# Adding the feed forward's residual with accumulating DMAs that queue behind GpSimd's gate products

## The chip, the cores and the metric

One core of a Trainium2 chip runs the whole program. Its engines are TensorE (PE, with its weight loads as PEld), VectorE (DVE), ScalarE (ACT), GpSimd (POOL) and SyncE (SP); each works off a queue of its own, in order. The metric is device time in microseconds, lower is better; it is the median of several executions.

## The reference, cut to what matters

Two layers work on 512 latent tokens of 1024 features (and 256 context tokens in layer 0). Each layer ends in a feed forward whose result is gated, feature by feature, and added to the residual:

```python
x = x + g1 * y
x = x + g2 * swiglu(modulate(x, norm_ffn_g[i], sh2, sc2), ffn_w_gate[i], ffn_w_up[i], ffn_w_down[i])
# swiglu(h) = (silu(h @ w_gate) * (h @ w_up)) @ w_down, with 2816 hidden features
```

In layer 0 the context tokens take the same path with gates of their own. In layer 1 a final RMSNorm follows.

## The kernel before

Every float32 product is made of three float32r products of high and low parts (`mm3`, L149 to L151). The feed forward's 2816 hidden features are 22 blocks of 128, numbered m = 0 to 21, and are made in pairs. A pair m, m + 1 goes through `up_strassen`: `W.strassen` loads four weight tiles (two of the gate matrix, two of the up matrix) into the ring `raw` of four buffers, GpSimd makes sums and differences in place in them (L116 to L119, one set of four for the gate matrix and one for the up matrix), and ScalarE and VectorE split each into a high part (L106) and a low part (L107). That gives seven left factors for each matrix. TensorE multiplies them into `p`, twelve matmuls for each factor; VectorE adds the products up in `a` (L888). Then ScalarE takes the silu, and L891 multiplies by the up half: for the first m of a pair on GpSimd, for the second on VectorE. `parts` splits the result for the down product (L842, L843).

The down product runs in sections: nine sections of one pair, then a last section of two pairs, m = 18 to 21. A section's sums `pd` are added by VectorE to an accumulator that stays in SBUF (L931). In the last section the first four sums begin with m = 18 and 19 alone ("the ahead groups": 24 matmuls that don't need the last pair), and each finished sum goes to `finish`, where it is gated and added.

Between the pairs, `between(m)` is called. At m = 18, behind the products of that pair in the program text and ahead of the last pair (20, 21), the kernel turns the accumulator of the nine sections into gate times accumulator plus residual. This is `ada_between` in layer 0 (L944, six tiles of 128 x 1024, the residual loaded from DRAM into the ring `raw`) and `settle` in layer 1 (L1435, four tiles, the residual in SBUF). Each tile takes a product on GpSimd (L951, L1438) and a sum on VectorE (L952, L1439). In layer 0, blocks of 16 small products for the modulation of layer 1 (`ada`, L230) fill TensorE between the pairs; their weights use the ring `raw` as well.

The order of every engine's queue is laid down when the program is built, by a planner that plays the program through on a model and, of the instructions that are ready for an engine, takes the one that stands first in the program text. From the last section's down product on, TensorE keeps the order of the text (`on_pe`). What the planner laid down does not change on the chip: an engine whose next instruction isn't ready waits.

Of the kernel before, what the change touches and what calls it, by code (L numbers as in the profile page):

```python
# [9 lines left out]
F32 = mybir.dt.float32  # L10
F32R = mybir.dt.float32r
AF = mybir.ActivationFunctionType
ALU = mybir.AluOpType
AX = mybir.AxisListType
PSUM = bass.MemoryType.PSUM

P = 128
# [37 lines left out]
class Weights:  # L55
    """Streams [128, 1024] weight units from DRAM and splits each into two float32r parts."""
# [5 lines left out]
    def slot(self):  # L62
        """[128, 1024] of the pools in turn"""
        pool, tag = self.pools[self.at // 2 % len(self.pools)], ("whi", "wlo")[self.at % 2]
        self.at += 1
        return pool.tile([P, 1024], F32R, tag=tag, name=f"w{self.at}")
# [28 lines left out]
    def strassen(self, pairs, order, eng):  # L95
        """The seven left factors of Winograd's form of Strassen's product, each [128, 512] in two parts, for pairs of units whose halves
        are the blocks (A11, A12) and (A21, A22); allotted in the given order of (pair, factor)"""
# [30 lines left out]
def kernel(ctx: ExitStack, tc: tile.TileContext, x, c, ctx_in, c_ctx, ada_w, ada_b,  # L128
# [24 lines left out]
    # constants and vectors  # L153
# [57 lines left out]
    def ada_steps(layer, ja, jb, ch, pp, slots=None):  # L211
        """256 features of two of the six parts of silu(c) @ ada_w + ada_b, feature on the partition of mod[layer, j].
        Column group k % 4 of the array sums the products of every fourth k."""
# [47 lines left out]
    def rms(xt, junk, n, name):  # L261
        """1 / sqrt(mean of squares + eps) of each row"""
# [13 lines left out]
    def norm_steps(xt, v, layer, j, dst, name):  # L276
        """modulate(xt) with parts j (shift) and j + 1 (scale), transposed, in two float32r parts: dst, each [128, 8, 128],
        or lists of its halves. First the norm, then the turning, in two halves"""
# [23 lines left out]
    def norm_later(*a):  # L302
        """the norm now, the turning when turn_oldest comes to it"""
        g_ = norm_steps(*a)
        next(g_)
        lag.append(g_)
# [6 lines left out]
    def on_pe():  # L313
        """from here the tensor engine keeps to the order in which its instructions are given"""
# [12 lines left out]
    class PP:  # L327
        """One PSUM pool under several tags."""
# [21 lines left out]
    # the first norm and the keys and values, as the shift and scale of each 256 features come in  # L350
# [16 lines left out]
    def h_chunk(ch):  # L367
        """features 256 * ch and on of the modulated, transposed tokens"""
# [50 lines left out]
    def rope(ps, t, nh, name):  # L419
        """rotated rows of a [128, nh*64] PSUM block"""  # L420
# [21 lines left out]
    def kv_evac(t):  # L442
        """keys (rotated) and values of token tile t out of PSUM, the keys in two float32r parts, each twice"""
# [9 lines left out]
    def k_turn(t, pools):  # L453
        """and turned"""
# [65 lines left out]
    def scores(t, b, h0, nh):  # L520
        """steps: masked scores of nh heads from h0 on of half b, query tile t, with the sink's logit behind them, and their maximum"""
# [39 lines left out]
    def weights(t, b, h0, nh):  # L561
        """their softmax weights"""
# [18 lines left out]
    def values(t, b, h0, nh):  # L581
        """their weighted values, feature on the partition: steps that turn the weights of some keys and steps that use them"""
# [45 lines left out]
    # what fills the array between the units: the coming queries and the modulation of the feed forward  # L628
# [115 lines left out]
    def add_gated(xt, ps, gate, hf, tmp, name):  # L744
        """xt[:, half] += gate * ps"""
# [5 lines left out]
    class Blocks:  # L751
        """The transposed tokens in 2 x 2 blocks (halves of the features, halves of the tokens, tile by tile), [128, 4, columns], each in
        two float32r parts; then what Winograd's form of Strassen's product takes in place of one of them, and three more"""
# [18 lines left out]
        def factors(self, more, tmp):  # L772
            """the seven right factors: B11, B21, B22 stay, more takes three, and B12 - B11, kept in the first two of tmp,
            is to take the place of B12"""
# [52 lines left out]
    def ffn(layer, h, extra, acc, xt, gate, es, sections, order, between, up_done, finish, mid):  # L827
# [18 lines left out]
        def up_first():  # L846
            """the first two m, one half of the tokens before the other"""
# [22 lines left out]
        def up_strassen(m):  # L870
            """m and m + 1: of each product's four blocks the first is P1 + P2, the second P1 + P6 + P5 + P3, the third P1 + P6 + P7 + P4,
            the fourth P1 + P6 + P7 + P5"""
# [16 lines left out]
            for x_, (g_, u_) in enumerate(a):  # L889
                nc.scalar.activation(out=g_, in_=g_, func=AF.Silu)  # L890
                (nc.vector if x_ else nc.gpsimd).tensor_tensor(out=u_, in0=u_, in1=g_, op=ALU.mult)  # L891
# [3 lines left out]
        for si, size in enumerate(sections):  # L895
# [22 lines left out]
            # the last section's first groups begin with the older half of the features  # L918
# [14 lines left out]

    es_x = ExitStack()
# [9 lines left out]
    def ada_between(m):  # L944
        if m == 4:
            G2.extend(load_gate(0, 5, 2))
        if m == 18:
            for e, t in enumerate((4, 5, 0, 1, 2, 3)):
                r = raw.tile([P, D], F32, tag="raw", name=f"xr_{t}")
                nc.sync.dma_start(out=r, in_=x_mid[t])  # L950
                nc.gpsimd.tensor_tensor(out=xt[t], in0=xt[t], in1=G2[0 if t < NL else 1], op=ALU.mult)  # L951
                nc.vector.tensor_tensor(out=xt[t], in0=xt[t], in1=r, op=ALU.add)  # L952
# [5 lines left out]
    def after_attention(e):  # L958
        """the turning of the last tiles behind the first products that don't need them"""
# [73 lines left out]
    def dt_step():  # L1033
        """step sizes of every head, their running sums along each chunk and what follows from them"""
# [434 lines left out]
```

## Time and profile before

| | us |
|---|---|
| three executions | 1975.98, 1976.86, 1983.81 |
| median | 1976.86 |
| span of the profiled execution | 1982.3 |
| longest of the three, the only one above that span | 1983.81 |
| TensorE busy | 1868.1 |
| VectorE busy | 1377.4 |
| GpSimd busy | 740.0 |

The span is the time from the first instruction to the last of one profiled execution. Of the times shown only 1983.81 can hold a span of 1982.3, so that is taken as its own time, with 1.5 us around the span. The feed forward of layer 0 ends its last pair at about 895 to 934 us, that of layer 1 at about 1920 to 1953 us.

### The profile page before, as it was taken

How to read it: one execution, taken by the hardware profiler on the slowest of the kernel's cores; microseconds unless marked ns; L12 is line 12 of the kernel's file. 1: busy time of each engine (PE TensorE's matmuls, PEld its weight loads, DVE VectorE, ACT ScalarE, POOL GpSimd, SP SyncE). 2: the span in 40 equal slices, each digit the busy share in tenths (PEclk: the TensorE clock that was granted, in tenths of full speed). 3: DMA queues.
4: the chain of work that ended last, by engine and by line, in shares of the span. 5: the costliest groups of instructions: out<-in, count | busy, mean ns of one | idle time of the engine just before them, and what ended most of it. 6: DMA issues, size and time to landing. Idle time of an engine off the chain costs nothing.

```text
span 1982.3 us, 29492 instructions
## 1 busy us (share of the span) xinstructions
PE 1868.1 (94%) x11168; PEld 1586.5 (80%) x11168; DVE 1377.4 (69%) x2359; ACT 894.2 (45%) x1607; POOL 740.0 (37%) x688
## 2 busy tenths in 40 slices
PE   6999998999999999989999999989989989999987
PEld 3777766889888888878888878777767888999877
DVE  4656655484666666687758777787777587787886
ACT  4675555344222222223556545665462454344333
POOL 1010002243333333364405545444545244535364
PEclk8999999999999999999999999999989999999989
DMA  9302137332333333344523332323243324332321
GB/s 303 119 1 86 43 98 240 121 117 86 106 107 106 107 107 107 107 132 144 162 75 110 96 87 81 112 85 105 85 157 103 113 86 123 91 107 85 107 59 70
DMA packets 226717, 214.88 MB, mean 108 GB/s; under 512 B 10352, under 2 KB 195152, under 8 KB 226576
## 3 DMA queue, kind: packets, MB, share of 16 engines
q1 hardware_dynamic: 214304, 189.56, 31.6%
q10 hardware_dynamic: 12272, 23.44, 3.4%
q8 instruction: 88, 1.44, 0.3%
q14 instruction: 53, 0.43, 0.1%
HBM read 201.27 MB, written 11.70 MB: 107 GB/s over the span
## 4 chain that ended last, share of the span: by engine, by line
PE 47%; DVE 16%; POOL 10%; DMA 10%; issue 9%; ACT 6%; ACTq 0%; POOLq 0%; DVEq 0%; SPq 0%
DVE w L107 4%; DMA R<-cum_rows 3%; PE p L149 3%; PE p L151 3%; PE p L150 3%; PE pd L149 3%; PE pd L150 2%; PE pd L151 2%; PE po L612 2%; POOL al L843 2%; DVE w L84 2%; PE ptp L596 2%; DMA raw<-in_ffn_w_gate_dram 2%; PE ada L230 2%; POOL raw L116 1%
## 5 line engine op out<-in xcount | busy, mean ns | idle before, releaser
L107 DVE TENSOR_TENSOR w<-raw,w 128x512 fp32r<-128x512 f32 x280 | 265.6, 962 | 138.8 <-ACT w L106 138.2
L106 ACT CAST w<-raw 128x512 fp32r<-128x512 f32 x280 | 166.2, 619 | 372.7 <-POOL raw L117 111.0
L149 PE MATMUL pd<-w,ah 128*128 128x512 f32 x440 | 175.1, 398 | 13.6 <-DVE y L931 9.0
L84 DVE TENSOR_TENSOR w<-raw,w 128x1024 fp32r<-128x1024 f32 (+1 forms) x117 | 152.2, 1304 | 34.0 <-ACT w L83 33.4
L150 PE MATMUL pd<-w,ah 128*128 128x512 f32 x440 | 173.5, 394 | 0.0
L83 ACT CAST w<-raw 128x1024 fp32r<-128x1024 f32 (+1 forms) x121 | 126.1, 1045 | 100.3 <-DMA raw<-in_ffn_w_down_dram 31.7
L151 PE MATMUL pd<-w,al 128*128 128x512 f32 x440 | 162.1, 394 | 4.2 <-POOL al L843 4.2
L149 PE MATMUL p<-hF_lh,w 128*128 128x256 f32 x384 | 110.7, 290 | 13.5 <-DVE ah_f L888 10.2
L149 PEld LDWEIGHTS pd<-w,ah 128*128 128x128 f32 x440 | 83.2, 189 | 35.6 <-DVE y L931 12.1
L116 POOL TENSOR_TENSOR raw<-raw 128x512 f32<-128x512 f32 x40 | 62.4, 1559 | 132.0 <-DVE w L107 126.1
L151 PE MATMUL p<-hF_lh,w 128*128 128x256 f32 x384 | 109.4, 285 | 0.0
L150 PE MATMUL p<-hF_ll,w 128*128 128x256 f32 x384 | 109.4, 286 | 0.0
L891 POOL TENSOR_TENSOR al_f<-al_f,ah_f 128x768 f32<-128x768 f32 (+1 forms) x20 | 35.2, 1759 | 186.6 <-DVE al_f L888 186.6
L151 PEld LDWEIGHTS pd<-w,al 128*128 128x128 f32 x440 | 82.6, 189 | 21.4 <-POOL al L843 4.8
L150 PEld LDWEIGHTS pd<-w,ah 128*128 128x128 f32 x440 | 83.3, 189 | 15.4
L118 POOL TENSOR_TENSOR raw<-raw,raw 128x512 f32<-128x512 f32 x40 | 56.1, 1402 | 97.6 <-DVE w L107 84.8
L843 POOL TENSOR_TENSOR al<-al_f,ah 128x768 fp32r<-128x768 f32 (+1 forms) x40 | 72.8, 1821 | 45.3 <-ACT ah L842 45.3
L888 DVE TENSOR_TENSOR al_f<-p,al_f 128x384 f32<-128x384 f32 (+1 forms) x140 | 66.1, 484 | 32.2 <-PE p L151 32.1
L149 PEld LDWEIGHTS p<-hF_lh,w 128*128 128x128 f32 x384 | 74.8, 196 | 15.5 <-DVE ah_f L888 11.4
L888 DVE TENSOR_TENSOR ah_f<-p,ah_f 128x384 f32<-128x384 f32 (+1 forms) x140 | 65.6, 484 | 26.4 <-PE p L151 23.6
L579 ACT COPY ph<-ptp 128x512 f32<-128x512 f32 (+1 forms) x96 | 52.9, 551 | 61.0 <-PE ptp L596 60.5
L149 PE MATMUL pz<-w,hD_lh 128*128 128x256 f32 x256 | 78.3, 306 | 0.0
(473 smaller groups left out, 6036.1 us busy)
## 6 DMA issues: line engine op xcount, KB each, us to landing
ar<-in_ada_w_dram SPq DMA_DIRECT2D x192, 256.0 KB, 4.3
raw<-in_ssm_w_in_dram SPq DMA_DIRECT2D x48, 512.0 KB, 4.1
raw<-in_ffn_w_gate_dram SPq DMA_DIRECT2D x44, 512.0 KB, 3.9
raw<-in_ffn_w_up_dram SPq DMA_DIRECT2D x44, 512.0 KB, 4.9
raw<-in_ffn_w_down_dram SPq DMA_DIRECT2D x44, 512.0 KB, 3.6
R<-cum_rows SPq DMA_DIRECT2D x32, 512.0 KB, 5.2
raw<-in_ssm_w_out_dram SPq DMA_DIRECT2D x16, 512.0 KB, 3.8
raw<-in_attn_w_qkv_dram SPq DMA_DIRECT2D x12, 512.0 KB, 6.0
```

The source lines that it names most:

```text
L83: nc.scalar.copy(out=hi[:, :n], in_=t[:, :n])
L84: (eng or nc.vector).tensor_tensor(out=lo[:, :n], in0=t[:, :n], in1=hi[:, :n].bitcast(F32), op=ALU.subtract)
L106: nc.scalar.copy(out=hi, in_=src)
L107: nc.vector.tensor_tensor(out=lo, in0=src, in1=hi.bitcast(F32), op=ALU.subtract)
L116: eng.tensor_tensor(out=a22, in0=a21, in1=a22, op=ALU.add)
L118: eng.tensor_tensor(out=a11, in0=a22, in1=a11, op=ALU.subtract)
L149: nc.tensor.matmul(ps, lhsT=ah, rhs=bh, start=start, stop=False)
L150: nc.tensor.matmul(ps, lhsT=ah, rhs=bl, start=False, stop=False)
L151: nc.tensor.matmul(ps, lhsT=al, rhs=bh, start=False, stop=stop)
L579: nc.scalar.copy(out=dst, in_=src)
L843: (nc.vector if (layer, m) in ((0, 18), (1, 20)) else nc.gpsimd).tensor_tensor(out=al, in0=u_, in1=ah.bitcast(F32), op=ALU.subtract)
L888: nc.vector.tensor_tensor(out=to, in0=ps, in1=other, op=ALU.add)
```

## The change

The products of GpSimd stay. The sums leave VectorE: each becomes a DMA issued from GpSimd's queue that adds the residual into the accumulator tile, from DRAM in layer 0 and from SBUF in layer 1. The six loads of the residual into the ring `raw` on SP's queue go. Products and DMA issues stand in a block that is queued on GpSimd behind the latest product of L891 on that engine, which is the one of m = 18. In layer 1 `xt` then names the tiles of the accumulator.

```diff
             for x_, (g_, u_) in enumerate(a):
                 nc.scalar.activation(out=g_, in_=g_, func=AF.Silu)
-                (nc.vector if x_ else nc.gpsimd).tensor_tensor(out=u_, in0=u_, in1=g_, op=ALU.mult)
+                ins = (nc.vector if x_ else nc.gpsimd).tensor_tensor(out=u_, in0=u_, in1=g_, op=ALU.mult)
+                if not x_:
+                    behind.append(ins.ins)
             return parts(a, m)
...
+    def gate_and_add(accs, gate, src):
+
+        with tc.issue_after(behind[-1]):
+            for a_, g_, s_ in zip(accs, gate, src):
+                nc.gpsimd.tensor_tensor(out=a_, in0=a_, in1=g_, op=ALU.mult)
+                nc.gpsimd.dma_start(out=a_, in_=s_, accum_op=ALU.add)
...
         if m == 18:
-            for e, t in enumerate((4, 5, 0, 1, 2, 3)):
-                r = raw.tile([P, D], F32, tag="raw", name=f"xr_{t}")
-                nc.sync.dma_start(out=r, in_=x_mid[t])
-                nc.gpsimd.tensor_tensor(out=xt[t], in0=xt[t], in1=G2[0 if t < NL else 1], op=ALU.mult)
-                nc.vector.tensor_tensor(out=xt[t], in0=xt[t], in1=r, op=ALU.add)
+            ts = (4, 5, 0, 1, 2, 3)
+            gate_and_add([xt[t] for t in ts], [G2[0 if t < NL else 1] for t in ts], [x_mid[t] for t in ts])
...
     def settle(m):
         if m == 18:
-            for t in range(NL):
-                nc.gpsimd.tensor_tensor(out=ys[t], in0=ys[t], in1=G2[0], op=ALU.mult)
-                nc.vector.tensor_tensor(out=xt[t], in0=xt[t], in1=ys[t], op=ALU.add)
+            gate_and_add(ys, [G2[0]] * NL, xt)
+            xt[:] = ys
```

`tc.issue_after(ins)` orders what the block puts on the engine of `ins` behind it in that engine's queue; it adds no wait. The rest of the diff takes comments out and changes no instruction.

## Rows read from the trace of the kernel before

**Rows 1.** The page: busy us, share of the span and instructions of each engine.

```profile
PE 1868.1 (94%) x11168; PEld 1586.5 (80%) x11168; DVE 1377.4 (69%) x2359; ACT 894.2 (45%) x1607; POOL 740.0 (37%) x688
```

**Rows 2.** TensorE in order of time: start us, us, instruction, [idle before <-releaser].

```profile
880.70 0.69 PE L149 MATMUL p<-h_4h,w 128*128 128x384 f32 x1 [3.02 <-ACT al_f L885]
...
898.62 0.34 PE L151 MATMUL p<-h_6h,w 128*128 128x384 f32 x1
898.89 1.92 PE L230 MATMUL ada<-ar,cs 128*32 128x512 f32 x16
...
1909.57 0.38 PE L149 MATMUL p<-hF_5h,w 128*128 128x256 f32 x1 [2.17 <-DVE al_f L888]
...
1918.87 0.58 PE L149 MATMUL p<-hF_lh,w 128*128 128x256 f32 x1 [7.56 <-DVE ah_f L888]
...
1930.82 0.28 PE L151 MATMUL p<-hF_6h,w 128*128 128x256 f32 x1
```

**Rows 3.** Windows: stretch, its length, busy us (instructions) of each engine, granted clock, DMA.

```profile
880.70:883.60 2.90, 2.90 (x9) 2.90 (x10) 2.90 (x5) 0.00 (x0) 0.00 (x0) 0.50 0.86 275
...
926.00:933.00 7.00, 7.00 (x42) 7.00 (x41) 3.44 (x6) 1.46 (x2) 1.84 (x1) 1.00 0.69 224
...
1910.00:1920.00 10.00, 2.44 (x16) 2.19 (x15) 10.00 (x9) 0.00 (x0) 5.73 (x4) 0.55 0.00 0
1918.87:1924.87 6.00, 6.00 (x28) 6.00 (x29) 5.74 (x9) 1.17 (x3) 5.76 (x4) 0.51 0.01 3
1930.00:1940.00 10.00, 10.00 (x85) 9.87 (x84) 6.55 (x10) 4.92 (x9) 9.28 (x6) 1.00 0.46 147
```

**Rows 4.** GpSimd in order of time, layer 0.

```profile
862.05 13.13 POOL L951 TENSOR_TENSOR y<-y,gate 128x1024 f32<-128x1024 f32 x5 [1.69 <-DVE y L931]
875.14 2.27 POOL L118 TENSOR_TENSOR raw<-raw,raw 128x512 f32<-128x512 f32 x1
...
895.54 1.85 POOL L891 TENSOR_TENSOR al_f<-al_f,ah_f 128x768 f32<-128x768 f32 x1 [15.93 <-DVE al_f L888]
899.22 1.28 POOL L116 TENSOR_TENSOR raw<-raw 128x512 f32<-128x512 f32 x1 [1.83 <-DVE w L107]
...
911.26 1.29 POOL L116 TENSOR_TENSOR raw<-raw 128x512 f32<-128x512 f32 x1 [5.12 <-DVE w L107]
```

**Rows 5.** The same of layer 1.

```profile
1899.95 5.74 POOL L1438 TENSOR_TENSOR ys<-ys,gate 128x1024 f32<-128x1024 f32 x2
1909.26 2.39 POOL L1438 TENSOR_TENSOR ys<-ys,gate 128x1024 f32<-128x1024 f32 x1 [3.57 <-DVE ys L931]
1915.21 2.72 POOL L1438 TENSOR_TENSOR ys<-ys,gate 128x1024 f32<-128x1024 f32 x1 [3.56 <-DVE ys L931]
1918.55 1.28 POOL L116 TENSOR_TENSOR raw<-raw 128x512 f32<-128x512 f32 x1 [0.63 <-DVE w L107]
...
1928.02 1.61 POOL L891 TENSOR_TENSOR al_f<-al_f,ah_f 128x512 f32<-128x512 f32 x1 [2.36 <-DVE al_f L888]
...
1931.89 1.74 POOL L116 TENSOR_TENSOR raw<-raw 128x512 f32<-128x512 f32 x1
```

**Rows 6.** VectorE in order of time, layer 1.

```profile
1899.95 6.90 DVE L107 TENSOR_TENSOR w<-raw,w 128x512 fp32r<-128x512 f32 x4
...
1913.85 0.68 DVE L107 TENSOR_TENSOR w<-raw,w 128x512 fp32r<-128x512 f32 x1
```

**Rows 7.** The lines that the change touches: engine op xcount: ns min/median/max, first and last start.

```profile
L952 DVE TENSOR_TENSOR y<-y,xr x6: 1208/1212/3423, 872.8 to 887.0; 128x1024 f32<-128x1024 f32 x6
L1439 DVE TENSOR_TENSOR xs_ctx_hi<-xs_ctx_hi,ys x2: 1209/1210/1211, 1907.4 to 1912.1; 128x1024 f32<-128x1024 f32 x2
L950 SPq DMA_DIRECT2D xr<-x_mid x6: 319/320/343, 853.1 to 882.0; - x6
DMA to landing us min/median/max: 3.2/3.4/4.8
```

**Rows 8.** SP's queue in order of time.

```profile
886.79 3.20 SPq L72 DMA_DIRECT2D raw<-in_ffn_w_gate_dram  x2
```

More of the change, by code (lines that the diff above doesn't have):

```diff
@@ L824 @@
     slots = [(raw, "raw"), (raw, "raw"), (w1, "whi"), (w2, "wlo")]
+    behind = []
     def ffn(layer, h, extra, acc, xt, gate, es, sections, order, between, up_done, finish, mid):
```

## The prediction

> **What bounds the kernel now.** I read the page first: TensorE is busy for 94% of the span, VectorE for 69%, GpSimd for 37% [rows 1]. So a time that changes is TensorE waiting more or less, or running at another clock; work that leaves VectorE counts for nothing by itself. Next I read TensorE in order of time around the changed lines, for idle time ahead of an instruction. In layer 0 there is one wait of 3.02 us behind the gate products; in layer 1 there are two, of 2.17 and 7.56 us [rows 2]. The windows show what follows such a wait: from 880.70 to 883.60 the granted clock is 0.50, that is 1.2 GHz, and nine matmuls take 2.90 us; from 1918.87 to 1924.87 it is 0.51, and 28 matmuls take 6.00 us [rows 3]. At 2.4 GHz the same shapes go at 7.00/42 = 0.17 and 10.00/85 = 0.118 us [rows 3]. So the slow matmuls cost 9 x (0.32 - 0.17) = 1.4 us and 28 x (0.214 - 0.118) = 2.7 us. All that hangs on this step is then 3.0 + 1.4 = 4.4 us in layer 0 and 2.2 + 7.6 + 2.7 = 12.4 us in layer 1, 16.8 us together.
>
> Who makes TensorE wait? In layer 0, GpSimd: L118 of the second set of factors of pair 18 starts at 875.14, right behind five gate products that take 13.13 us [rows 4]. In layer 1, VectorE: it is busy for all 10 us of 1910 to 1920 [rows 3], with the residual sums, 1.21 us and more each [rows 7], and with remainders (L107) that take 6.90 us for four beside two gate products, where one takes 0.68 us by itself [rows 6]. The next products need a PSUM buffer, which VectorE empties in its turn.
>
> **What the change takes away.** Ten sums leave VectorE: six of 1.21 us and more in layer 0, four in layer 1 [rows 7], 12.1 us at least. On their own they are worth nothing; they are part of the waits above. Six loads leave SP's queue and the ring of four weight buffers. The last of them is issued at 882.0 [rows 7], and the gate weights of the last pair only at 886.79 [rows 8]. I expect these weights some 10 us earlier or more, and so the first set of factors of the last pair, L116 at 899.22 in layer 0 [rows 4], ahead of L891 of pair 18. That is no gain of its own, since TensorE reaches those factors later, but it decides what stands behind the gate products.
>
> **What it moves.** The gate products go behind L891 of pair 18, at 895.54 in layer 0 and 1928.02 in layer 1 [rows 4, 5]. They are ready there at once, and of the ready instructions the planner takes the one that stands first in the text. So all of them, each with its DMA issue, come ahead of GpSimd's sums for the last pair that are not ready by then. In layer 1 the second set of these starts at 1931.89, behind L891 [rows 5]; in layer 0 it starts at 911.26, behind L891 as well [rows 4]. I take it that this second set stays behind and so waits for the whole block.
>
> **What a DMA issue costs GpSimd.** No row shows a DMA issued by GpSimd. Below, the bound is an issue on SP, 0.32 us; above, the time in which such a transfer lands, 3.4 us [rows 7], as if GpSimd were held to the end. I take 1.3 us, the length of one half-width instruction on GpSimd (1.28 us) [rows 4]: it is work for that engine over 128 partitions, but not a pass over a tile. The issues cost 6 x 1.3 = 7.8 us in layer 0 and 4 x 1.3 = 5.2 us in layer 1.
>
> The transfers themselves lie beside other work. Even if an adding transfer took three times the 3.4 us, one behind the other, the fourth tile of layer 1 would be there at about 1917 + 2.6 + 41 + 4 = 1965 us, about when the final sums reach it. I cost them at nothing; that cover is thin, and only in layer 1.
>
> **Layer 0, step by step.** All comes 4.4 us earlier: L891 ends at 895.54 + 1.85 - 4.4 = 893.0. Six products of 13.13/5 = 2.63 us [rows 4] and the issues take 15.8 + 7.8 = 23.6 us, to 916.6. Then L116 and L117 (2.6 us) and one split on ScalarE and VectorE (1.3 us) give the first factor of the second set at 920.5. TensorE ends pair 18 at 898.9 - 4.4 = 894.5 [rows 2]. Without the second set it has: the modulation block of 1.92 us [rows 2], nine factors of twelve matmuls (four that need no sums, five of the first set), 9 x 12 x 0.17 = 18.2 us, and the 24 matmuls of the ahead groups, 512 columns for 384, 24 x 0.23 = 5.5 us. That lasts to 920.1, so the wait is 0.4 us. The last five factors take 10.1 us, to 930.6. Now nothing is left to cover the way of the last pair to its down product: I estimate two passes on GpSimd of 1.85 us and ScalarE's between them as 5 us. So the last down products begin at 935.6. Before, the same work ran through with the ahead groups as cover: 898.9 + 1.9 + 28.3 + 5.5 = 934.6. Layer 0 loses 1.0 us: what it gains at pair 18 it gives back at the last pair.
>
> **Layer 1.** L891 ends at 1928.02 + 1.61 - 12.4 = 1917.2. Then come two remainders L843 (2.6 us), four gate products (5.74 + 2.39 + 2.72 = 10.9 us [rows 5]) and the issues (5.2 us): 1935.9. The factor is there 3.9 us later, at 1939.8. TensorE ends pair 18 at 1931.1 - 12.4 = 1918.7 [rows 2], has 9 x 1.42 = 12.8 us of factors and 24 x 0.236 = 5.7 us of ahead groups, to 1937.2, and waits 2.6 us. The last five factors take it to 1946.9, the uncovered way (narrower tiles, 4 us) to 1950.9. Before: 1931.1 + 19.9 + 5.7 = 1956.7. Layer 1 gains 5.8 us of its 12.4.
>
> **The sum** is 5.8 - 1.0 = 4.8 us. I add 1 us for two waits on late weights in layer 0 that should go with the loads, which is a guess of its own: 5.8 us. The profiled execution would go from 1983.8 (span 1982.3) to 1978.0, the median from 1976.9 to 1971. That the profiled execution is 7 us above the median is not explained by these rows; a part of the waits may be peculiar to it.
>
> With an issue at 0.32 us, layer 0 keeps its 4.4 us and layer 1 about 9.7 us: 1963. At 3.4 us, layer 0 loses another 12.6 us and layer 1 another 8.4 us: 1992.
>
> **The contention goes along.** Beside two gate products four remainders took 6.90 us instead of 4 x 0.68 = 2.7 us [rows 6]: 2.1 us of VectorE for each gate product. The ten products are not removed, and where they go VectorE makes remainders for the last pair. If a fourth of 10 x 2.1 = 21 us reaches TensorE through late PSUM buffers, the gain is gone. I count none in the sum, since VectorE has fewer sums there (6.55 of 10 us busy from 1930 to 1940 [rows 3]).
>
> The Trainium skill, "SBUF — State Buffer", section "Who interferes with whom", says that a VectorE instruction with two inputs in SBUF contends with a GpSimd instruction that reads SBUF; the trace agrees with the 6.90 us above, and by that rule the price moves with the products, which would put the time at the rival of no change below. The Trainium skill, "DMA: Bandwidth & Descriptors", section "SWDGE vs HWDGE vs iDMA", says that an accumulating DMA can be issued from GpSimd only and that GpSimd's cores compute its descriptors; no run here shows it yet, and its figure for a transfer (2.0 us and bytes over 436e3, an estimate of 3.2 us for these tiles) would change nothing in the sum.
>
> **The rivals.** *Full gain*: the second set gets ahead of the block, or an issue costs next to nothing, so that only the waits go: 1976.9 - 16.8 = 1960. For it: in layer 0 the second set starts 12 us behind the end of L891, for lack of weights that will be there sooner. Against it: in layer 1 it stood behind L891 without a gate product between. *No change*: the waits of VectorE move with the contention: 1977. For it speak the remainders in rows 6. *Slower*: the block of products and issues on GpSimd becomes the bound of the last pair. Each microsecond of an issue above 1.3 costs 6 us in layer 0 and 4 us in layer 1, so beyond 1.9 us an issue the change loses; at a gate product's own length, 2.6 us, it loses 7 us: 1984. Against it speaks only that an issue moves no data on GpSimd.
>
> **How the numbers follow.** Faster or slower by 0.5% (9.9 us, about what a measurement of this kernel tells from no change) is below 1967 or above 1986.7. Forecast, a part of the gain near 1971: 0.42; full gain near 1960: 0.25; no change near 1977: 0.16; slower, near 1984: 0.17. Faster: all of the full gain and a quarter of the forecast, 0.35. Slower: the upper part of the slow case, beyond 2.9 us an issue, and what the planner may lay out worse elsewhere, 0.13. The rest, 0.52, is within the bound. The range of 8 in 10 goes from 1958, the full gain and a little, to 1986, the slow case at 2.8 us an issue.
>
> **What would show it.** In the changed kernel the gate products start at about 893 and 1917 us, right behind L891 of pair 18, with gaps between them that are the issue's cost; L118 of pair 18 starts without a gate product ahead; the waits of 3.02 and 7.56 us and the stretches at 1.2 GHz are gone; the second set of the last pair starts 20 us and more behind L891, with a wait of TensorE of 0 to 3 us ahead of its factors. The forecast is wrong if an issue holds GpSimd for over 1.9 us, if the second set stands ahead of the products, if a transfer lands after the final sums ask for it, or if VectorE's remainders beside the products hold PSUM as they do now.

## The result: 0.8% slower

The changed kernel takes 1994.66 us (median of 5 runs, 1992.24 to 2000.27), the kernel before 1976.86 us (1973.08 to 1984.89) on the same chip: a ratio of 1.0082, interval 1.0059 to 1.0106 (the quotient of the medians is 1.0090; the ratios in this text are those on record). The forecast was 1971 us in a range of 1958 to 1986. The profiled execution took 2000.27 us, span 1998.5 us, 16.2 us more than the span before; it lies 5.6 us above its median, as the one before lay 7.0 us above its own. Of the 16.2 us about 12 come in layer 0's feed forward (its first turned tile for the scan is made at 971.5 us for 958.1, and its start was already 1.6 us late) and about 3.5 us in layer 1's; 0.7 us are made up in between.

TensorE of the changed kernel in order of time, the instructions ahead of which it stood still, and the last one ahead of the longest stop:

```profile
895.75 1.92 PE L230 MATMUL ada<-ar,cs 128*32 128x512 f32 x16
...
904.81 0.44 PE L151 MATMUL p<-h_0h,w 128*128 128x384 f32 x1 [2.42 <-DVE w L107]
...
911.21 1.12 PE L237 MATMUL ada<-ident,adasb 128*128 128x128 f32 x4 [5.07 <-DVE adasb L233]
...
926.84 0.69 PE L149 MATMUL p<-h_5h,w 128*128 128x384 f32 x1 [5.19 <-ACT w L106]
...
1938.47 0.28 PE L151 MATMUL p<-hF_5h,w 128*128 128x256 f32 x1
1952.62 0.58 PE L149 MATMUL p<-hF_5h,w 128*128 128x256 f32 x1 [13.86 <-ACT w L106]
```

The waits of 3.02, 2.17 and 7.56 us at pair 18 [rows 2] are gone: the modulation block of pair 20 starts at 895.75 for 898.89, on a run that started 1.6 us later. In their place stand four new waits in the last pair, 26.5 us together. Windows of the changed kernel (stretch, its length, then busy us and instructions of PE, PEld, DVE, ACT, POOL, the granted clock, DMA) show the gain and where it is given back:

```profile
866.00:900.00 34.00, 34.00 (x196) 31.34 (x195) 22.95 (x30) 9.87 (x16) 15.15 (x9) 1.00 0.27 78
900.00:930.00 30.00, 17.31 (x75) 16.29 (x74) 21.56 (x20) 8.11 (x13) 23.61 (x15) 0.72 0.70 154
...
911.30:917.00 5.70, 5.70 (x20) 5.70 (x21) 4.95 (x7) 1.44 (x3) 5.54 (x5) 0.51 0.47 69
...
1938.60:1952.60 14.00, 0.15 (x2) 0.00 (x0) 0.51 (x3) 0.62 (x1) 13.00 (x11) 0.58 0.59 126
...
1952.60:1960.00 7.40, 7.38 (x42) 7.39 (x43) 6.56 (x7) 3.56 (x5) 2.28 (x2) 0.64 0.84 189
926.80:940.00 13.20, 13.16 (x63) 12.77 (x64) 10.49 (x12) 4.19 (x5) 2.29 (x2) 0.86 0.87 255
```

Up to 900 us TensorE is full; then it has work for 17 of 30 us, and what it does from 911.3 to 917 it does at 0.51 of full speed, the lower level of 1.2 GHz, after standing still. In layer 1 hardly anything but GpSimd works for 14 us. Behind both waits for the second set TensorE again works a while at the lower level. What GpSimd does there, first layer 0, then layer 1:

```profile
893.28 2.29 POOL L893 TENSOR_TENSOR al_f<-al_f,ah_f 128x768 f32<-128x768 f32 x1
895.53 17.23 POOL L942 TENSOR_TENSOR y<-y,gate 128x1024 f32<-128x1024 f32 x6
912.71 2.00 POOL L943 DMA_DIRECT2D y<-x_mid  x2
914.06 1.95 POOL L116 TENSOR_TENSOR raw<-raw 128x512 f32<-128x512 f32 x1
915.29 1.55 POOL L943 DMA_DIRECT2D y<-x_mid  x1
918.52 0.88 POOL L943 DMA_DIRECT2D y<-x_mid  x1 [1.68 <-issue]
921.07 0.86 POOL L943 DMA_DIRECT2D y<-x_mid  x1 [1.66 <-issue]
923.99 0.86 POOL L943 DMA_DIRECT2D y<-x_mid  x1 [2.06 <-issue]
924.55 1.59 POOL L117 TENSOR_TENSOR raw<-raw,raw 128x512 f32<-128x512 f32 x1
...
1931.68 10.85 POOL L942 TENSOR_TENSOR ys<-ys,gate 128x1024 f32<-128x1024 f32 x4
...
1950.33 1.58 POOL L117 TENSOR_TENSOR raw<-raw,raw 128x512 f32<-128x512 f32 x1
```

The products begin right behind L893 (L891 before [rows 4, 5]), 2.87 and 2.71 us each. Then come the issues; from the fourth on GpSimd stands still for 1.7 to 2.1 us ahead of each in layer 0, and for 0.92 us ahead of the fourth in layer 1. Behind all of them stands L117 of the last pair's second set of factors, 29 us and 19 us after the first product. The transfers themselves, from the group of L943 in the view by lines:

```profile
L943 POOL DMA_DIRECT2D y<-x_mid x6: 857/982/1554, 912.7 to 924.0; - x6
...
DMA to landing us min/median/max: 4.6/7.6/9.8
```

### The profile page after: what moved, and what is told of

Read it like the earlier page. It is cut to its first block, busy times and chain, and to the rows that moved or that the text cites. A ratio compares the mean times of both kernels' runs of the same rounds, so it can differ in the third digit from the quotient of the medians.

```text
span 1998.5 us, 29502 instructions
## 1 busy us (share of the span) xinstructions
PE 1870.5 (94%) x11168; PEld 1588.3 (79%) x11168; DVE 1361.2 (68%) x2349; ACT 894.7 (45%) x1607; POOL 744.3 (37%) x698
## 4 chain that ended last, share of the span: by engine, by line
PE 38%; DVE 18%; POOL 14%; DMA 12%; issue 11%; ACT 6%; ACTq 0%; POOLq 0%; DVEq 0%; SPq 0%
DMA R<-cum_rows 4%; DVE w L107 4%; DMA raw<-in_ffn_w_gate_dram 3%; DVE w L84 3%; POOL al L845 2%; PE po L612 2%; PE pd L149 2%; DMA raw<-in_ffn_w_down_dram 2%; PE pd L150 2%; PE ptp L596 2%; PE pd L151 2%; POOL raw L117 2%; POOL raw L116 2%; POOL al_f L893 2%; ACT w L106 1%
## 5 line engine op out<-in xcount | busy, mean ns | idle before, releaser
L107 DVE TENSOR_TENSOR w<-raw,w 128x512 fp32r<-128x512 f32 x280 | 260.6, 943 | 163.9 <-ACT w L106 162.9
L106 ACT CAST w<-raw 128x512 fp32r<-128x512 f32 x280 | 166.4, 619 | 388.6 <-POOL raw L117 123.2
L83 ACT CAST w<-raw 128x1024 fp32r<-128x1024 f32 (+1 forms) x121 | 125.9, 1044 | 106.8 <-DMA raw<-in_ffn_w_down_dram 28.1
L116 POOL TENSOR_TENSOR raw<-raw 128x512 f32<-128x512 f32 x40 | 62.6, 1564 | 144.4 <-DVE w L107 141.4
L893 POOL TENSOR_TENSOR al_f<-al_f,ah_f 128x768 f32<-128x768 f32 (+1 forms) x20 | 35.7, 1783 | 174.5 <-DVE al_f L890 174.5
L890 DVE TENSOR_TENSOR al_f<-p,al_f 128x384 f32<-128x384 f32 (+1 forms) x140 | 66.1, 484 | 34.6 <-PE p L151 34.3
L845 POOL TENSOR_TENSOR al<-al_f,ah 128x768 fp32r<-128x768 f32 (+1 forms) x40 | 73.0, 1825 | 43.9 <-ACT ah L844 43.9
L890 DVE TENSOR_TENSOR ah_f<-p,ah_f 128x384 f32<-128x384 f32 (+1 forms) x140 | 65.4, 484 | 27.4 <-PE p L151 24.3
L935 DVE TENSOR_TENSOR y<-pd,y 128x512 f32<-128x512 f32 x96 | 63.1, 682 | 22.1 <-PE pd L151 22.1
```

The source lines that it names most:

```text
L83: nc.scalar.copy(out=hi[:, :n], in_=t[:, :n])
L106: nc.scalar.copy(out=hi, in_=src)
L107: nc.vector.tensor_tensor(out=lo, in0=src, in1=hi.bitcast(F32), op=ALU.subtract)
L116: eng.tensor_tensor(out=a22, in0=a21, in1=a22, op=ALU.add)
L845: (nc.vector if (layer, m) in ((0, 18), (1, 20)) else nc.gpsimd).tensor_tensor(out=al, in0=u_, in1=ah.bitcast(F32), op=ALU.subtract)
L890: nc.vector.tensor_tensor(out=to, in0=ps, in1=other, op=ALU.add)
```

## The experiments

Three theories. **A**: the block of products and issues on GpSimd delays the second set of the last pair's factors, and TensorE, whose order was laid down for an earlier second set, has too little to do meanwhile. **B**: the issues with their gaps are the cost. **C**: the products hold VectorE back where it now makes the last pair's remainders. In all runs that are compared, the time of the kernel before is that of the same chip: 1977.93 us for "products alone", "not queued", "another order" and "sums back on VectorE", 1979.38 for "the same order in the kernel before", "half the scratch memory" and the two kernels in which products and issues alternate, 1979.26 for the four with products on VectorE.

**Products alone** (the DMAs out; the residual is left out of the result).

```diff
                 nc.gpsimd.tensor_tensor(out=a_, in0=a_, in1=g_, op=ALU.mult)
-                nc.gpsimd.dma_start(out=a_, in_=s_, accum_op=ALU.add)
```

> The changed kernel without the ten accumulating DMAs: the residual of both feed forwards is left out, all else is as in the changed kernel. Theory A (the second set of factors of the last pair waits on GpSimd for the block of products and issues, and TensorE's laid-down order has nothing to cover it): L117 of that set comes some 10 us earlier in layer 0 and 3 us earlier in layer 1, the wait of 5.2 us in layer 0 goes, that of 13.9 us in layer 1 shrinks to 10 to 11, time near 1985. Theory B (the issues, not the products, are the cost): both waits go, time at or below 1978. Theory C (VectorE is held up beside the products): the two waits of 2.4 and 5.1 us of layer 0 stay as they are.

Measured: 1980.35 us, 1.0006 of before (0.9994 to 1.0018), 14.3 us less than the change. TensorE keeps two waits in layer 0, 2.38 us on L107 and 5.10 us on L233, as with the DMAs, and in layer 1 9.40 of the 13.86 us; the 5.19 us are gone. TensorE, then GpSimd, in layer 1:

```profile
1933.01 0.58 PE L149 MATMUL p<-hF_5h,w 128*128 128x256 f32 x1 [9.40 <-ACT w L106]
```

```profile
1931.04 1.27 POOL L117 TENSOR_TENSOR raw<-raw,raw 128x512 f32<-128x512 f32 x1
```

TensorE stops ahead of the same factor as in the changed kernel, the second set's hF_5, with the same work behind it. So the issues are worth 14 us, but not the two waits on VectorE, and two thirds of the long wait stand without them.

**Not queued** (products and DMAs where the planner puts them by itself).

```diff
-        with tc.issue_after(behind[-1]):
+        if True:
             for a_, g_, s_ in zip(accs, gate, src):
```

> The accumulating DMAs kept, the queueing behind the products of pair 18 taken away, so that products and issues go where the planner likes, about where the products were before the change. Theory A: no wait at the last pair (13.9 and 5.2 us go); in layer 0 the wait ahead of L118 of pair 18 comes back and is longer by the issues, 5 to 12 us; in layer 1 the sums of VectorE are gone and the waits of 2.2 and 7.6 us shrink to half or less; time 1970 to 1982. Theory B: the issues cost the same wherever they stand, time 1988 or more.

Measured: 1975.86 us, 0.9995 (0.9979 to 1.0012), as theory A expected: without the queueing the change isn't slow. The planner now lets products and issues alternate ahead of pair 18's own sums, and of the waits of before 2.21 us in layer 0 and 1.05 and 6.48 us in layer 1 are still there, on VectorE. The longer wait in layer 0 that theory A expected, 5 to 12 us, didn't come.

**Another order of the last pair's factors** (the four that need no sums, all of the first set, then all of the second).

```diff
             seq = [(i, j) for j0 in ((1, 2), (6, 7), (5, 3), (4,)) for i in range(2) for j in j0]
+            if m == 20:
+                seq = [(i, j) for i in range(2) for j in (1, 2)] + [(i, j) for i in range(2) for j in (6, 7, 5, 3, 4)]
```

> The changed kernel with another order of TensorE's products in the last pair alone: after the four factors that need no sums come all five others of the first set, then the five of the second. Theory A: three more factors (4.3 us in layer 1, 6.2 us in layer 0) lie under the delay, so the wait in layer 1 goes from 13.9 to about 9.6 us and that in layer 0 from 5.2 to 0, time near 1986. Theories B and C, if the cost is not the missing cover: no change, 1994.

Measured: 1986.67 us, 1.0045 (1.0027 to 1.0062), 8 us less than the change. The time is the one that theory A expected, but not for its reason. The wait of 13.86 us is gone because in layer 1 GpSimd now makes the second set ahead of L895, the product that the block is queued behind:

```profile
1920.01 1.63 POOL L117 TENSOR_TENSOR raw<-raw,raw 128x512 f32<-128x512 f32 x1
...
1926.03 1.60 POOL L895 TENSOR_TENSOR al_f<-al_f,ah_f 128x512 f32<-128x512 f32 x1 [1.03 <-DVE al_f L892]
1927.59 12.26 POOL L944 TENSOR_TENSOR ys<-ys,gate 128x1024 f32<-128x1024 f32 x4
```

The edit changes not only TensorE's order: `W.strassen` also allots the factors' buffers in it, and the planner laid GpSimd's queue down anew. So in layer 1 this run doesn't test whether more factors ahead cover the block. In layer 0, where the block still stands ahead of the second set and five factors of the first set do run ahead of it, waits of 4.35 us (L233) and 4.91 us (L106) stay, 9.3 us for the 12.7 us of the changed kernel; that the second would go was a miss. In layer 1 waits of 1.96 and 2.79 us, on VectorE and ScalarE, are new.

**The same order in the kernel before.**

> The kernel before, with nothing of the change but the order of the last pair's factors of the run that took 8 us off the changed kernel. Theory A: the order is worth something only where GpSimd comes late with the second set; before the change it does not, so 1977 us, within 0.3%. Rival, the order is better by itself: 8 us less, 1969 us.

Measured: 1983.03 us, 1.002 (1.0004 to 1.0036): no better, if anything 4 us worse. The order is worth 8 us only together with GpSimd's block.

**Half the scratch memory for descriptors.**

```diff
-    nc = bacc.Bacc("TRN2", target_bir_lowering=False, num_devices=1, dynamic_dma_scratch_size=1024)
+    nc = bacc.Bacc("TRN2", target_bir_lowering=False, num_devices=1, dynamic_dma_scratch_size=512)
```

> The changed kernel with half the scratch memory for the descriptors of GpSimd's DMAs (512 for 1024). Theory R, the gaps of 1.7 to 2.1 us that follow the third accumulating DMA come from this ring being full until an earlier DMA has been taken out of it: with half of it they begin one or two issues earlier, and are longer, since the wait is now for the DMA just before. At least two more gaps of 2 us in layer 0 and two in layer 1: 8 us more on GpSimd, which the second set of the last pair hands on to TensorE, near 2002 us. Rival, the gaps have nothing to do with the ring (each is the chip working off earlier descriptors): the same gaps at the same issues, 1994.7 us.

Measured: 2018.27 us, 1.02 (1.0178 to 1.0221), 23.6 us more than the change. GpSimd in layer 0:

```profile
906.50 1.07 POOL L943 DMA_DIRECT2D y<-x_mid  x1
912.14 0.89 POOL L943 DMA_DIRECT2D y<-x_mid  x1 [4.56 <-issue]
...
923.07 0.88 POOL L943 DMA_DIRECT2D y<-x_mid  x1 [4.68 <-issue]
928.55 0.86 POOL L943 DMA_DIRECT2D y<-x_mid  x1 [4.59 <-issue]
933.88 0.88 POOL L943 DMA_DIRECT2D y<-x_mid  x1 [4.47 <-issue]
```

Now the second issue waits already, and the issues follow each other by 5.3 to 5.6 us, about as long as one of these transfers takes to land here (4.5 to 5.5 us): one at a time. TensorE waits 20.25 us in layer 0 and 23.65 us in layer 1 for the second set. Theory R holds and its size was short (2002 expected): GpSimd stands at the issue until an earlier transfer is through.

**Sums back on VectorE, products queued.**

```diff
-        with tc.issue_after(behind[-1]):
-            for a_, g_, s_ in zip(accs, gate, src):
+        for a_, g_, s_ in zip(accs, gate, src):
+            if len(accs) == 6:
+                r = raw.tile([P, D], F32, tag="raw", name=f"xr_{a_.tensor.name}")
+                nc.sync.dma_start(out=r, in_=s_)
+                s_ = r
+            with tc.issue_after(behind[-1]):
                 nc.gpsimd.tensor_tensor(out=a_, in0=a_, in1=g_, op=ALU.mult)
-                nc.gpsimd.dma_start(out=a_, in_=s_, accum_op=ALU.add)
+            nc.vector.tensor_tensor(out=a_, in0=a_, in1=s_, op=ALU.add)
```

> The queueing kept, the DMAs undone: the products stand behind those of pair 18, and VectorE adds the residual as before the change (loads into the weight ring in layer 0). Theory A: nearly as slow as with the DMAs, since the products alone delay the second set: a wait of about 10 us at the last pair in layer 1, time 1984 to 1992. Theory B: no issue, so no loss, time 1977 or below.

Measured: 2006.68 us, 1.0138 (1.0116 to 1.016), worse than the change and than the 1984 to 1992 us that theory A expected. Its wait at the last pair of layer 1 did come: 11.97 us, where about 10 were expected, without any issue. Neither theory expected what came in layer 0: TensorE waits 22.86 us there for a load of the modulation weights: the residual's tiles hold the ring of four weight buffers until the late products are done. With a queue this late the DMAs into the accumulator are the better way for the residual.

**Products and issues alternate**, still queued; and the same **with the other order**.

```diff
-        with tc.issue_after(behind[-1]):
-            for a_, g_, s_ in zip(accs, gate, src):
-                nc.gpsimd.tensor_tensor(out=a_, in0=a_, in1=g_, op=ALU.mult)
-                nc.gpsimd.dma_start(out=a_, in_=s_, accum_op=ALU.add)
+        last = behind[-1]
+        for a_, g_, s_ in zip(accs, gate, src):
+            with tc.issue_after(last):
+                p_ = nc.gpsimd.tensor_tensor(out=a_, in0=a_, in1=g_, op=ALU.mult).ins
+            with tc.issue_after(p_):
+                last = nc.gpsimd.dma_start(out=a_, in_=s_, accum_op=ALU.add).ins
```

> The changed kernel, still queued behind the 18th pair, but each product behind the issue of the tile before, so that products and issues alternate, and the sums of the last pair's second set get in between. Theory A (block on GpSimd without cover on TensorE): L117 of the second set comes after three products instead of six and six issues in layer 0, about 908 us for 924.6, and after two products in layer 1, about 1943 for 1950; no gap of over 1 us is left at the issues, as each has 2.9 us of a product behind it. TensorE's wait of 5.2 us in layer 0 goes, that of 13.9 us in layer 1 falls to about 5: 5 us and 9 us less, and what goes on behind the block some 5 more: 1976 to 1980 us. Theory B, an issue costs GpSimd 2 us or more wherever it stands (it waits for the transfer before): the gaps stay, the block is as long, and the time stays above 1988 us.

> As the run with products and issues alternating, and with the last pair's factors laid out as in the run with the other order of the last pair (the four that need no sums, then all of the first set, then all of the second). Theory A: the order took 8 us off, the alternation takes off what the block still holds back in layer 0 (4.9 us there) and the rest of the wait in layer 1: 1972 to 1980 us, no slower than before the change. Theory C, what is left is VectorE's contention with the products, which alternation only spreads: two waits of 2 to 5 us in layer 0 stay and the time is 1980 us or more.

Measured: 2003.24 us, 1.0116 (1.01 to 1.0132), and with the order 1992.5 us, 1.0061 (1.0044 to 1.0079). The first is slower than without the alternation; the second is not to be told from the other order alone (1.0045, 1.0027 to 1.0062). Theory A's 1976 to 1980 and 1972 to 1980 us were missed. Theory C's expectation for the second (two waits in layer 0, 1980 us or more) came true, with waits of 6.01 and 5.51 us. In the first the gaps at the issues did go, and L117 of the second set came at 908.8 us for 924.6, as theory A had it. But VectorE and GpSimd in the first of the two:

```profile
906.59 16.53 DVE L107 TENSOR_TENSOR w<-raw,w 128x512 fp32r<-128x512 f32 x1 [1.35 <-ACT w L106]
...
906.45 2.72 POOL L943 TENSOR_TENSOR y<-y,gate 128x1024 f32<-128x1024 f32 x1
908.81 1.60 POOL L117 TENSOR_TENSOR raw<-raw,raw 128x512 f32<-128x512 f32 x1
...
919.09 3.48 POOL L943 TENSOR_TENSOR y<-y,gate 128x1024 f32<-128x1024 f32 x1
```

One remainder that takes 0.68 us by itself [rows 6] takes 16.53 us, from the third product to the end of the last at 922.6; TensorE's wait is 11.58 us, on VectorE's L890 behind it, and in layer 1 two waits of 5.64 and 5.48 us stand for the 13.86. In the other run it is a pass over 128x4 elements that takes 13.39 us. So theory C is right in kind, and the longest holds seen stand where products, sums and issues follow each other without a break.

**Products on VectorE**, DMAs on GpSimd; without the queue, with it, and with queue and other order.

```diff
-                nc.gpsimd.tensor_tensor(out=a_, in0=a_, in1=g_, op=ALU.mult)
+                nc.vector.tensor_tensor(out=a_, in0=a_, in1=g_, op=ALU.mult)
                 nc.gpsimd.dma_start(out=a_, in_=s_, accum_op=ALU.add)
```

> The changed kernel without the queueing behind the 18th pair, and with the gate products on VectorE instead of GpSimd; the accumulating DMAs stay on GpSimd. Theory C (GpSimd's products hold VectorE back while they run, up to 16.5 us for one remainder of 0.68 us where they follow each other closely): with no product on GpSimd the waits on VectorE of the run that was not queued (2.2 and 1.0 us in layer 0, 1.1 and 6.5 us in layer 1) shrink to under 3 us together: 1966 to 1972 us, against 1975.9 for the same with GpSimd's products. Theory A (only GpSimd's block counts, VectorE is not the point): the ten products of 1.2 us take the place of the ten sums on VectorE, and the time is that of before, 1977 us.

> The changed kernel, queued as it is, with the gate products on VectorE. GpSimd's block is then the issues alone, six of about 2 us in layer 0 and four of about 1.3 us in layer 1. Theory C: TensorE's waits on VectorE in layer 0 (2.4 and 5.1 us) go, those for the second set fall from 5.2 to 0 and from 13.9 to about 5 us, and VectorE's own 1.2 us a product give some 3 us back: 16 to 19 us less, 1976 to 1979 us. Theory B (the issues and their gaps are the cost, the products are not): the waits on VectorE stay, and only the second set comes earlier: 1984 to 1988 us.

> The run before this one with the other order of the last pair's factors (the four without sums, all of the first set, all of the second). Theory A: what is left of the wait for the second set in layer 1 has the first set's factors ahead of it and goes: 1968 to 1974 us, ahead of the kernel before. Theory B, as the issues in layer 0 still stand between the first and the second set: no better than without the order.

Measured: without the queue 1968.51 us, 0.9939 (0.9917 to 0.996), faster than both kernels and within theory C's 1966 to 1972; with it 1981.58 us, 1.001 (0.9994 to 1.0025); with queue and order 1978.53 us, 1.0 (0.9985 to 1.0016). Without the queue TensorE has one wait of over 2 us left around the change; the product ahead of it takes VectorE 1.2 us:

```profile
1905.42 0.58 PE L149 MATMUL p<-hF_lh,w 128*128 128x256 f32 x1 [3.68 <-DVE al_f L890]
```

```profile
1903.82 1.21 DVE L942 TENSOR_TENSOR ys<-ys,gate 128x1024 f32<-128x1024 f32 x1
```

With the queue only the issues stand behind L893, since it orders GpSimd alone; VectorE makes the products at 858 to 872 us as in the run without. GpSimd, then TensorE, in layer 0 of the queued run:

```profile
893.83 2.87 POOL L943 DMA_DIRECT2D y<-x_mid  x3
899.45 0.88 POOL L943 DMA_DIRECT2D y<-x_mid  x1 [2.75 <-issue]
905.32 0.86 POOL L943 DMA_DIRECT2D y<-x_mid  x1 [5.00 <-issue]
907.98 0.86 POOL L943 DMA_DIRECT2D y<-x_mid  x1 [1.80 <-issue]
...
913.86 0.69 PE L149 MATMUL p<-h_4h,w 128*128 128x384 f32 x1 [5.78 <-ACT w L106]
```

Three issues go out at once, the fourth waits, and TensorE's waits for the second set are 5.78 us here and 5.96 us in layer 1 (the 0 and 5 of theory C's expectation missed the gaps at the issues, here 4.26 us in layer 1 as well; the time lies between what C and B expected). Beside the issues VectorE's remainders take their 0.68 us and its L893 0.95 us: issues alone don't hold VectorE back. The 2.42 and 5.07 us on VectorE are gone. The edits of these two runs differ only in the queueing, and so in where the issues stand, and that is 13.1 us; the queued one and the change differ only in the engine of the products, and that is 13 us by the times, 14 by the ratios. The order takes 3 us more off, which the intervals don't tell apart. Theory A's 1968 to 1974 us for it are a miss: waits of 6.23 us in layer 0 and 4.62 us in layer 1 remain, now put down to VectorE's L892 (L890 in the other runs), and in layer 0 VectorE itself has stood still for 9.34 us shortly ahead of it, for a split of the second set. So TensorE's new order doesn't help where VectorE's queue has the second set ahead, and the queued version doesn't get ahead of the kernel before.

**The kernel before with its products on VectorE** (sums and loads as they were).

```diff
-                nc.gpsimd.tensor_tensor(out=ys[t], in0=ys[t], in1=G2[0], op=ALU.mult)
+                nc.vector.tensor_tensor(out=ys[t], in0=ys[t], in1=G2[0], op=ALU.mult)
```

(and the same line of layer 0.)

> The kernel before with nothing changed but the engine of the ten gate products, VectorE instead of GpSimd. Theory C: each product on GpSimd costs VectorE about 2.1 us of being held back and on VectorE 1.2 us of its own, so VectorE gains some 9 us in the two stretches in which TensorE waits for it, and the time falls by 3 to 9 us, to 1968 to 1974 us. Rival: VectorE is full in layer 1 from 1910 to 1920 and another 5 us of products there lengthen TensorE's wait of 7.6 us: 1980 us or more.

Measured: 1976.62 us, 0.9986 (0.9971 to 1.0002), 2.6 us less and not to be told from nothing: less than theory C's 3 to 9, and not the 1 us more of its rival. What VectorE is no longer held back it spends on the products. Only with the sums gone to DMAs as well does the time fall.

## Why the prediction was wrong

**The gains were right.** Layer 0's wait and layer 1's two are gone. The modulation block starts at 895.75 us for 898.89 [rows 2] on a start 1.6 us later: 4.7 us gained for the 4.4 predicted. The last hF_6 product of pair 18 ends at 1930.2 us for 1931.1 [rows 2], though layer 1's feed forward began 12.7 us later: 13.6 us. Of these 0.8 us are no gain, since seven matmuls of the next pair stood ahead of that product before and stand behind it now; so 12.8 us for 12.4.

**The block was right in place and kind, and longer in layer 0.** The products stand behind pair 18's L893 at once, and the second set behind all of them: as forecast. The first set of layer 0's last pair starts 12 us earlier than before (L116 at 887.21 us for 899.22 [rows 4]), ahead of L893: as forecast too. In layer 1 the forecast had the first factor of the second set at 1939.8 us; with the 12.7 us later start of the layer that is 1952.5, and TensorE takes it up at 1952.62. That it fits so closely is in part luck: L893 ends 1.8 us later than forecast, and against that the issues cost 4.2 us (from 1944.90 to L117 at 1950.33, less 1.2 us of L845 among them) where 5.2 were set, and the other pieces are 0.6 us shorter. In layer 0 the factor came 4.7 us later than 920.5 and 1.6 of late start: 1.0 us of it is the later end of L893, 1.4 the products (17.2 us for 15.8), 2.8 the issues, less 0.4 for the sums and the split. The issues cost 10.6 us (912.71 to 924.55, less 1.2 us of L116) where 7.8 were set: an issue alone was mostly below the 1.3 us (0.86 to 1.55 us, median 0.98), but from the fourth one GpSimd waits for an earlier transfer. The run with half the scratch memory shows this wait to hang on the room for descriptors. No row of before could have shown it. The section that was cited for the issue (the Trainium skill, "DMA: Bandwidth & Descriptors", section "SWDGE vs HWDGE vs iDMA") also says that GpSimd appends the descriptors to rings in SBUF. The trace agrees with a ring that has an end: three transfers fit here.

**The step that failed in layer 1 is the cover.** The prediction let TensorE run nine factors and the 24 products of the ahead groups before it needs the second set: "to 1937.2, and waits 2.6 us". TensorE keeps its laid-down order, and so do ScalarE and GpSimd. TensorE from the last pair's start on, then GpSimd and ScalarE:

```profile
1930.06 0.28 PE L149 MATMUL p<-hF_lh,w 128*128 128x256 f32 x1
...
1935.72 0.28 PE L149 MATMUL p<-hF_4h,w 128*128 128x256 f32 x1
...
1953.21 0.41 PE L149 MATMUL p<-hF_lh,w 128*128 128x256 f32 x1
...
1960.78 0.39 PE L149 MATMUL pd<-w,ah 128*128 128x512 f32 x1
```

```profile
1943.70 1.26 POOL L845 TENSOR_TENSOR al<-al_f,ah 128x512 fp32r<-128x512 f32 x1
...
1945.57 1.52 POOL L845 TENSOR_TENSOR al<-al_f,ah 128x512 fp32r<-128x512 f32 x1
```

```profile
1951.94 0.62 ACT L106 CAST w<-raw 128x512 fp32r<-128x512 f32 x1 [16.06 <-POOL raw L117]
...
1954.34 1.99 ACT L83 CAST w<-raw 128x1024 fp32r<-128x1024 f32 x2
```

Only six factors stand ahead: the four without sums, from 1930.06 us, and two of the first set, hF_4 and hF_5, to 1938.75 us; then comes the second set's hF_5 [1952.62 above]. Behind it stand the other three factors of the first set (3 x 1.42 = 4.3 us), split by 1930.6 us and so ready all the time, and the ahead groups (5.7 us). Of these not all could have run: their low parts (L845) are made on GpSimd at 1943.70 and 1945.57, behind the gate products, and of the four splits of down weights that they and the last pair need (L83) ScalarE made one at 1934.57 us and the others from 1954.34 us on, behind the second set's L106. Ten us of the counted cover are missing, and TensorE was done with pair 18 1.2 us earlier than forecast: 2.6 + 10.0 + 1.2 = 13.8 us, and the wait is 13.86 us. The run without issues shows the same stop: with the counted cover of 10 us its wait of 9.40 us wouldn't be there. A run in which TensorE's order alone is changed was not made; the run with the other order changed GpSimd's too.

The forecast also charged 5 us in layer 0 and 4 us in layer 1 for an uncovered way from the last pair to its down product. They didn't come: with ahead groups left over, TensorE goes on from the last factor without a stop (947.5 and 1969.4 us).

**In layer 0 the step that failed is the contention, set to nothing.** It "goes along", the prediction said, and counted none, because VectorE had fewer sums; the window that it cited for that is layer 1's. In layer 0 VectorE was nearly full at this place before the change:

```profile
900.00:930.00 30.00, 28.98 (x164) 26.79 (x157) 26.51 (x36) 13.27 (x20) 11.74 (x8) 1.00 0.55 167
```

VectorE of the changed kernel there, beside the gate products:

```profile
904.68 3.11 DVE L893 TENSOR_TENSOR al_f<-al_f,ah_f 128x768 f32<-128x768 f32 x1
907.72 2.83 DVE L107 TENSOR_TENSOR w<-raw,w 128x512 fp32r<-128x512 f32 x1
910.47 0.68 DVE L233 COPY adasb<-ada 128x512 f32<-128x512 f32 x1
```

TensorE's waits on it are 2.42 + 5.07 = 7.5 us, which stay without the DMAs (2.38 and 5.10 us) and go with the products on VectorE; and with them goes half of the 5.7 us that TensorE then works at half speed, 2.8 us. The text said that a fourth of 21 us would cancel the gain; the waits alone are a third, all in layer 0. TensorE runs out of work there at 921.65 us, as forecast (920.1 and 1.6 of late start), by luck: the 10.3 us lost to VectorE took the time in which it would have done the three factors and the ahead groups that stand behind the second set here too. So the wait of 5.19 us, where 0.4 were forecast, is the 4.7 us by which the factor came later.

The Trainium skill, "SBUF — State Buffer", section "Who interferes with whom", says that a VectorE instruction with two inputs in SBUF contends with a GpSimd instruction that reads SBUF, and calls the port pair that the two engines share an exclusive lock. The traces agree that VectorE waits: beside the products of the changed kernel its passes with two inputs in SBUF take 2.1 to 3.1 us each, where they take 0.68 to 0.95 us beside issues alone, and L890, with one input in PSUM, keeps its 0.55 us. That one instruction can wait through four products, as in the 16.53 us, the section doesn't say, and why GpSimd lets VectorE in between two products but not between a product, a sum and an issue stays open.

**The sum.** Half speed after the waits for the second set costs 1.8 us more in layer 0 (13.2 us at 0.86) and 2.7 us in layer 1 (7.4 us at 0.64). Layer 0 is then -4.7 + 2.4 + 5.1 + 5.2 + 2.8 + 1.8 = 12.6 us, 11.8 measured; layer 1 is -12.8 + 13.9 + 2.7 = 3.8 us, 3.5 measured. Two readings of the rows were off and change nothing in the sum: in layer 0 the second set starts 13.9 us behind the end of L891, not 12 [rows 4], and the four remainders of 6.90 us [rows 6] lie ahead of the window from 1910 to 1920.

The rival "slower" was the one that came, by the mechanism it named, the block on GpSimd as the bound of the last pair (in layer 0 together with the contention, which was another rival's), but not at its price: it was tied to an issue of over 1.9 us, and in layer 1 it came with 1.1 us. The threshold was worked out from a cover that isn't there and without the contention; with both in the count nothing is left to gain at any price of an issue, since the products without issues already give 1.0006 of before.

**What doesn't add up.** The pieces overlap: issues out, 14 us less; products off GpSimd, 13 us less; the order, 8 us less; no queue, 19 us less; the excess is 18 us. All four shorten or take away the wait for the second set, and some of them the waits on VectorE too. These runs were made on different chips, whose times of the kernel before differ by up to 2.5 us; taken as ratios the four are 0.76, 0.72, 0.37 and 0.87% of the time, that is 15, 14, 7 and 17 us.

## What to carry to other kernels

Before counting a later engine's backlog as cover for a late operand, read in the trace in which order the waiting engine takes its work: what stands behind the late operand covers nothing, however ready it is, and the engines that feed that work may stand in a laid-down order of their own. Moving work off an engine that is the bound helps only where the place it goes to isn't ahead of something with less slack; here the same DMAs without the queue, with the products on VectorE, gave 0.6%; queued behind the pair they gave nothing, and queued with the products on GpSimd they lost 0.8%. And where a GpSimd pass and VectorE's two-input passes share time, price both: 2.9 us on GpSimd against 1.2 us on VectorE, and no VectorE instruction held.

## What the runs showed of the chip

- An accumulating DMA of 512 KB costs GpSimd 0.86 to 1.55 us to issue while there is room: with the products on VectorE and the queue, three go out one behind the other (2.87 us for three), the fourth waits 2.75 us and the fifth 5.00 us. With half the scratch memory each waits for the one before, 5.3 to 5.6 us apart.
- Such a transfer lands after 4.6 to 9.8 us, several in flight (median 7.6 us), where a plain load of the same size lands after 3.4 us [rows 7]. In the changed kernel no wait of TensorE or VectorE is put down to one of them.
- A VectorE pass of 128x4 elements was held for 13.39 us, and one of 128x512 for 16.53 us, while GpSimd made products, sums and issues without a break; both read two inputs from SBUF. Beside issues alone the pass of 128x512 takes 0.68 us.
